# Merging column-tiled matmul groups and ordering a one-core decoder-layer kernel for late transfers

## Chip, cores and metric

One core of one Trainium2 chip runs the kernel. The metric is device microseconds of one execution; the time before is the median of 3 runs. TensorE is PE in the profile, VectorE DVE, ScalarE ACT, GpSimd POOL, and SyncE, which starts every transfer of this kernel, SP.

## What is computed

One decoder layer in float32 for a prompt of 512 tokens and 8 single-token samples, 520 token columns in all. Cut to what matters:

```python
mod = silu(c) @ w_ada + b_ada                       # shift, scale, gate; twice
h = modulate(rmsnorm(x), sh_m, sc_m)
u, z, xbc, dt_raw, g_a, g_b = split(h @ w_in)
ya, s5 states = s5_mixer(u, ...)                    # diagonal complex recurrence, 64 groups of 16 channels
yb, ssm states = ssd_mixer(z, xbc, dt_raw, ...)     # 32 heads of 64, chunks of 128 tokens
merged = sigmoid(g_a) * (ya @ w_branch_s5) + sigmoid(g_b) * (yb @ w_branch_ssd)
x = x + gt_m * rmsnorm(merged @ w_out)
gu = modulate(rmsnorm(x), sh_f, sc_f) @ w_ffn_in
x = x + gt_f * rmsnorm((silu(gu[:, :F]) * gu[:, F:]) @ w_ffn_out)
```

All new states (S5, SSM, convolution; of the prompt and of each sample) are outputs too.

## The kernel before, in words

Features lie on the 128 partitions, tokens along the free dimension. The **main stream** is the list of weight tiles of `build` (line 900): u, dt, the gates, then B, C, xs and z of four groups, glu, the two branches, w_out, w_ffn_in (fg, fu) and w_ffn_out (fo). A weight chunk is 128 output features by up to 1024 input features, 128x1024 words. It is loaded by SP (`wload`, line 858), rounded by ACT into `whi` (`wsplit_hi`, 863), its rest goes by DVE into `wlo` (`wsplit_lo`, 882), and PE multiplies it block of features by block (`product`, 1148): six passes of 260 token columns, hi and lo of the input on `whi`, and hi on `wlo`, for each half of the tokens. A chunk of eight blocks is 48 such passes. `whi` and `wlo` have three buffers each, so the split of a chunk can't start before PE is through with the chunk three places earlier.

Around it runs **side work**, written as Python generators: the S5 mixer (`s5` and helpers, 1731 to 2093), the SSD mixer (`ssd_unit`, 2247: two heads at a time, 16 units), the samples' outputs (`ssd_y`, 2321), their new states (`ssd_state`, 2369: 32 times a load `in_ssm`, three DVE operations of 128x512, a store), the last modulation (`ada_last`, 1350), and norms.

Three kinds of side matmuls use only some columns of the array. Their outputs go to 64 or 32 partitions, and the column groups work side by side:
- a unit's output, 64 columns, 14 matmuls; lines 2355 and 2362 (`if c % 2 == 0` and `if c % 2`) gather them in two bunches, of 6 and of 8;
- the samples' outputs, 32 columns, 32 matmuls for each of four head groups, in four bunches of 8, each on a 512 KB load `in_ssmT` (two buffers);
- the last modulation, 32 columns and 512 wide, eight bunches of 2.
The S5 and early modulation set-up has some more. A float32 matmul is two passes on the array, so two records in the trace.

No operation is issued when its helper is called. `Plan.add` records it with an estimated cost (from `mm`, `dma`, `act_cost` and so on) and with the memory it touches. At the end `Plan.order` (275) makes many schedules: `play` (352) runs all operations on a model of the engines, each engine taking the most urgent that can start; `back` (315) derives new priorities from the schedule run backwards; 24 rounds add random shifts to the priorities. The schedule with the earliest modelled end,
```python
end = max(o.fin for o in ops)
```
is issued, so each engine's instruction order is fixed when the program is built, and each engine then takes its instructions strictly in that order. A `bunch` (743) is one operation for the planner: nothing comes between its matmuls.

Of the kernel before, what the change touches and what calls it, by code (L numbers as in the profile page):

```python
# [46 lines left out]
PSTEP = 1 << 32  # L47


class Root:  # L50
    """A tile: `get` gives the real one (it may be made late); `loc` names the memory it lies in."""
# [14 lines left out]
class Ap:  # L66
    """A view of a tile: its shape and addresses at once, the real view when the operation is issued."""
# [65 lines left out]
    def cells(self):  # L133
        """Partitions, and the set of words in one of them (bits of an integer)."""
# [35 lines left out]
class Op:  # L170
    __slots__ = ("eng", "cost", "fn", "deps", "fset", "xfer", "start", "fin", "n", "nm", "pos", "prio", "main", "boost", "lead", "alt", "home", "nwait", "succ", "ready")

    def __init__(self, eng, cost, fn, deps, fset, xfer, boost=0.0):
        self.eng, self.cost, self.fn, self.deps, self.fset, self.xfer = eng, cost, fn, deps, fset, xfer
        self.nm, self.main, self.boost, self.alt, self.home = 1, False, boost, None, None


# delay in us from the end of an operation to the start of one that waits for it
# [7 lines left out]
class Line:  # L186
    """The time of one engine: busy stretches, into whose gaps operations are put."""
# [24 lines left out]
class Plan:  # L212
    """Records operations with the memory they touch, and orders them for the engines."""
# [51 lines left out]
    def remake(self, loc, fn, words):  # L265
        """The memory `loc` gets a new tile: after everything that used the old one."""
# [8 lines left out]
    def order(self):  # L275
        """The best of some schedules: by the longest way to the end, then by latest starts."""
# [20 lines left out]
        for r in range(NPERT + 1):  # L297
# [7 lines left out]
            for i in range(3 if r else NFB + 1):  # L305
                done = self.play()
                end = max(o.fin for o in ops)
# [7 lines left out]
    def back(self):  # L315
        """Priorities from the schedule played backwards: the time from an operation's latest start to the end."""
# [9 lines left out]
        while n < len(ops):  # L326
# [19 lines left out]
            for p, d in o.deps.items():  # L346
                rdy[p] = max(rdy[p], x + d)
# [4 lines left out]
    def play(self):  # L352
        """The course of the operations, each engine taking the most urgent of those that can start."""
# [8 lines left out]
        fset, cols, seen, pos = None, {}, {}, dict.fromkeys("VAGPSX", 0)  # L362
# [4 lines left out]
        while len(done) < len(ops):  # L367
# [47 lines left out]
            done.append(o)  # L415
            for s, d in o.succ:
                s.ready = max(s.ready, o.fin + d )
# [4 lines left out]

    def shift(self, t, free, cand):
        """An operation of DVE that ACT may take at time t, where that is done sooner."""
# [32 lines left out]
class Arena:  # L457
    """One run of words in a tile of one type; blocks are cut out of it first fit."""
# [39 lines left out]
class Mem:  # L498
    """A fixed float32 arena, and slots whose type (float32 or float32r) is chosen when one is empty."""
# [10 lines left out]
    def find(self, n, dt, top):  # L510
        """The place for n words: an arena index (0 = the fixed one), or None."""
# [89 lines left out]
class Builder:  # L601
# [76 lines left out]
    def relu(self, o, a, s):  # L678
        """max(a + s, 0)"""
# [18 lines left out]
    def dma(self, o, a, boost=0.0):  # L698
        """Starts a transfer; returns the estimate of its end."""
# [9 lines left out]
        c = n / run * max(.4375e-3, run * (1 if run >= 512 else 2) / 360e3)  # L709
# [6 lines left out]
    def mm(self, o, l, r, start=True, stop=True):  # L716
        n, m = self.fs(r), l.shape[-1]
        if l.dtype == F32R:
            c = max(n / 2400, .111) if m > 32 else .048
        else:  # L720
            c = max(n * 4 / 2400, .216) * max(m, 32) / 128 + (.021 if m <= 64 else 0.0)
        self.pe(c, lambda: self.nc.tensor.matmul(real(o), lhsT=real(l), rhs=real(r), start=start, stop=stop),  # L722
                [o], [l, r])

    def idle(self, o, n, after=None):
        """Matmuls on zeros."""
# [1777 lines left out]
```

## Time and profile before

| what | us |
|---|---|
| median of 3 runs | 1204.94 |
| the 3 runs | 1200.02, 1204.94, 1205.42 |
| profiled execution, span from first to last instruction | 1193.2 |
| median minus that span | 11.7 |
| PE busy | 1168.8 (98%) |
| DVE busy | 814.7 (68%) |
| ACT busy | 576.3 (48%) |
| PE's share of the chain that ended last | 79% |

The page gives the span of the profiled execution, not its whole time; what lies around a span is the 11.7 us of the table if that execution was like the median one. A PE record of a 260-column pass lasts about 0.28 us, while the next pass starts about 0.12 us after it: passes overlap, so work on PE is counted here by starts. An idle time that the profile states for PE begins at the end of the last record.

### The profile page before, as it was taken

The numbers are of one execution on the slowest core, as the hardware profiler recorded it, in microseconds if no ns is written. First come the engines' busy times: TensorE is split into PE (matmuls) and PEld (weight loads), VectorE is DVE, ScalarE is ACT, GpSimd is POOL, SyncE is SP. The second block draws the span as 40 slices with busy tenths as digits, with TensorE's granted clock in tenths as the row PEclk, the third lists the DMA queues.
The fourth block names the chain that finished last, engine by engine and source line by source line (L and its number), as shares of the span: only waits on it lengthen the run. The fifth ranks groups of instructions, "written<-read, shape, count | busy, mean of one in ns | idle before, by whom it ended". The sixth has DMA issues, their size and how long they took to land.

```text
span 1193.2 us, 24814 instructions
## 1 busy us (share of the span) xinstructions
PE 1168.8 (98%) x10182; PEld 1124.5 (94%) x10182; DVE 814.7 (68%) x1651; ACT 576.3 (48%) x981; POOL 4.9 (0%) x32
## 2 busy tenths in 40 slices
PE   8999999999999999999999999999999899999998
PEld 6899898999999999999998989999999899999997
DVE  6898989997696877868885435499576673322236
ACT  6655444357487657847853323465223222222233
POOL 0000000000000000000000000000000000000000
PEclk9999999999999999999999999999999999999999
DMA  8838698667243343355545674344566663223244
GB/s 292 278 119 219 162 215 224 180 160 208 82 134 101 114 128 125 116 175 169 188 145 201 241 268 144 129 166 147 182 217 203 198 206 104 88 81 97 83 130 135
DMA packets 118066, 195.49 MB, mean 164 GB/s; under 512 B 45856, under 2 KB 68800, under 8 KB 115648
## 3 DMA queue, kind: packets, MB, share of 16 engines
q1 hardware_dynamic: 117952, 193.90, 52.9%
q8 instruction: 80, 1.31, 0.4%
q14 instruction: 34, 0.28, 0.1%
HBM read 165.81 MB, written 23.86 MB: 159 GB/s over the span
## 4 chain that ended last, share of the span: by engine, by line
PE 79%; DMA 9%; DVE 7%; issue 1%; SPq 1%; ACT 1%; DVEq 0%; ACTq 0%
PE pm L722 64%; PE bank L722 14%; DVE s L640 4%; DMA arena<-in_ssm 3%; DVE arena L640 2%; PE bank L734 2%; DMA s<-in_w_as 1%; DMA out_ssm_s<-arena 1%; SPq L712 1%; DVE wlo L640 1%; DMA s<-in_w_in 1%; DMA ud<-s 1%; DMA s<-s 1%; DVE s L663 1%; ACT s L696 0%
## 5 line engine op out<-in xcount | busy, mean ns | idle before, releaser
L722 PE MATMUL pm<-hi,whi 128*128 128x260 f32 (+1 forms) x1856 | 497.5, 289 | 5.9 <-DVE arena L640 3.7
L722 PE MATMUL pm<-lo,whi 128*128 128x260 f32 (+1 forms) x1856 | 483.4, 282 | 0.0
L722 PE MATMUL pm<-hi,wlo 128*128 128x260 f32 x1840 | 370.4, 283 | 0.0
L722 PEld LDWEIGHTS pm<-hi,whi 128*128 128x128 f32 (+1 forms) x1856 | 349.6, 188 | 17.4 <-issue 13.0
L722 PEld LDWEIGHTS pm<-lo,whi 128*128 128x128 f32 (+1 forms) x1856 | 349.1, 188 | 0.1
L640 DVE TENSOR_TENSOR wlo<-arena,whi 128x1024 fp32r<-128x1024 f32 (+1 forms) x157 | 188.8, 1203 | 146.7 <-ACT whi L696 144.9
L722 PEld LDWEIGHTS pm<-hi,wlo 128*128 128x128 f32 x1840 | 282.9, 188 | 0.0
L696 ACT CAST whi<-arena 128x1024 fp32r<-128x1024 f32 (+1 forms) x158 | 162.6, 1029 | 197.1 <-PE pm L722 180.2
L722 PE MATMUL pm<-s,whi 128*128 128x260 f32 (+2 forms) x1128 | 184.2, 283 | 0.0
L640 DVE TENSOR_TENSOR arena<-arena 128x512 f32<-128x512 f32 (+11 forms) x299 | 140.3, 494 | 49.8 <-DMA arena<-in_ssm 29.4
L722 PEld LDWEIGHTS pm<-s,whi 128*128 128x128 f32 x1128 | 156.2, 188 | 5.1 <-issue 4.2
L722 PE MATMUL pm<-s,wlo 128*128 128x260 f32 (+2 forms) x564 | 117.2, 283 | 0.0
L722 PEld LDWEIGHTS pm<-s,wlo 128*128 128x128 f32 x564 | 88.1, 188 | 0.0
L691 ACT ACT_TABLE_LOAD x63 | 80.8, 1283 | 10.3 <-DMA s<-acd 3.5
L722 PE MATMUL bank<-s,s 128*64 128x128 f32 (+5 forms) x672 | 75.8, 282 | 5.6 <-ACT s L696 4.4
L722 PEld LDWEIGHTS bank<-s,s 128*128 128x128 f32 (+2 forms) x672 | 61.3, 164 | 10.9 <-ACT s L696 5.3
L691 ACT ACTIVATE s<-s 128x520 f32<-128x520 f32 (+10 forms) x89 | 50.0, 570 | 38.3 <-DVE s L640 17.7
L691 ACT ACTIVATE arena<-pm 128x260 f32<-128x260 f32 (+3 forms) x44 | 21.2, 489 | 92.7 <-PE pm L722 85.7
L640 DVE TENSOR_TENSOR s<-arena,s 128x520 fp32r<-128x520 f32 (+5 forms) x60 | 56.5, 948 | 10.6 <-ACT s L696 10.4
L640 DVE TENSOR_TENSOR s<-s,arena 128x8 f32<-128x8 f32 (+6 forms) x138 | 48.6, 369 | 13.8 <-ACT s L691 12.7
L722 PE MATMUL bank<-hi,s 128*128 128x260 f32 x256 | 55.5, 285 | 0.0
L722 PE MATMUL pm<-hi,s 128*128 128x260 f32 x256 | 55.0, 285 | 0.0
(122 smaller groups left out, 1265.8 us busy)
## 6 DMA issues: line engine op xcount, KB each, us to landing
arena<-in_w_in SPq DMA_DIRECT2D x59, 512.0 KB, 3.7
arena<-in_w_fi SPq DMA_DIRECT2D x44, 512.0 KB, 4.4
arena<-in_w_ada SPq DMA_DIRECT2D x12, 1024.0 KB, 7.5
arena<-in_w_fo SPq DMA_DIRECT2D x20, 512.0 KB, 3.6
arena<-in_ssmT SPq DMA_DIRECT2D x16, 512.0 KB, 4.4
s<-acd SPq DMA_DIRECT2D x16, 512.0 KB, 4.3
arena<-in_w_bssd SPq DMA_DIRECT2D x16, 512.0 KB, 5.4
arena<-in_ssm SPq DMA_DIRECT2D x32, 256.0 KB, 3.8
```

The lines of the kernel that those rows point to most:

```text
L640: self.op("V", .068 + self.fs(o) / 960, lambda: self.nc.vector.tensor_tensor(out=real(o), in0=real(a), in1=real(b), op=op), [o], [a, b, *a ...
L663: self.op("V", .068 + self.fs(o) / 960, lambda: self.nc.vector.tensor_tensor_scan(out=real(o), data0=real(a), data1=real(b), initial=0.0, ...
L691: self.op("A", c, lambda: self.nc.scalar.activation(real(o), real(a), f, bias=real(bias), scale=real(scale)), [o], [a, scale, bias], None ...
L696: self.op("A", c, lambda: self.nc.scalar.copy(real(o), real(a)), [o], [a])
L712: p = self.op("S", .475 if same else .65, lambda: self.nc.sync.dma_start(out=real(o), in_=real(a)), [o], [a], None, c)
L722: self.pe(c, lambda: self.nc.tensor.matmul(real(o), lhsT=real(l), rhs=real(r), start=start, stop=stop), [o], [l, r])
L734: self.pe(.108, lambda: self.nc.tensor.transpose(real(o), real(a), real(d)), [o], [a, d])
```

## The change

It does four things. (1) The matmuls of a unit's output are one bunch of 14 instead of 6 and 8; those of the samples' outputs come in bunches of 16 instead of 8; those of the last modulation in bunches of 4 instead of 2. The two loads that feed a bunch of the latter two kinds are both waited for, and the next two are started after it. (2) The planner charges PE 0.09 us where the number of columns in use changes, and gives an operation with the same narrow tile a bonus of 4 us in urgency. (3) Estimates: a 260-column pass costs 0.120 us instead of 0.108, transfers go at 330 instead of 360 GB/s, and whoever waits for a transfer is planned 1 us later. (4) Of the schedules, the one with the best mean end over six rehearsals is taken, in which the order is fixed and each transfer is late by a random time of mean 0.5 us. The arithmetic, the transfers and the number of matmuls stay as they are.

```diff
+RATE = 330e3
+WAIT = 1.0
+LATE = .5
+NREH = 6
+NSW = .09
+TSTAY = 4.0
...
             for i in range(3 if r else NFB + 1):
                 done = self.play()
-                end = max(o.fin for o in ops)
+                end = self.rehearse(done)
...
             for p, d in o.deps.items():
-                rdy[p] = max(rdy[p], x + d)
+                rdy[p] = max(rdy[p], x + d + (WAIT if p.eng == "S" else 0.0))
...
+            elif e == "P":
+                o = max(c, key=lambda o: (o.prio + (TSTAY if o.tile == tile != 128 else 0.0), -o.n))
+                if o.tile != tile:
+                    t += NSW
+                    tile = o.tile
...
+            late = WAIT if e == "S" else 0.0
             for s, d in o.succ:
-                s.ready = max(s.ready, o.fin + d )
+                s.ready = max(s.ready, o.fin + d + late)
...
+    def rehearse(self, done):
...
+        for r in range(NREH):
+            rnd = random.Random(r)
+            fin, free, lanes = [], dict.fromkeys("VAGPSXQ", 0.0), [0.0] * 8
+            for e, c, deps, wt, load, xfer, lane in rows:
+                t = free[e] + load
...
+                if e == "S":
+                    t = max(t, dep, lanes[lane]) + c
+                    free[e] = t
+                    t = free["Q"] = max(free["Q"], t + .65) + xfer
+                    t += rnd.expovariate(1 / LATE)
+                    lanes[lane] = t + .95
+                else:
+                    t = max(t, dep + wt) + c
+                    free[e] = t
+                fin.append(t)
+            total += max(fin)
+        return total / NREH
...
-        c = n / run * max(.4375e-3, run * (1 if run >= 512 else 2) / 360e3)
+        c = n / run * max(.6e-3, run * (1 if run >= 512 else 3) / RATE)
...
-            c = max(n / 2400, .111) if m > 32 else .048
+            c = max(n * .441e-3 + .005, .112)
...
-        for n in range(8):
+        for n in range(1, 8, 2):
             e, q = 10 + n // 4, n % 4
-            yield ts[n % 2]
-            if q == 0:
+            yield max(ts)
+            if q == 1:
                 p = yield from self.pget()
             with self.bunch():
-                for i in range(2):
-                    j = 2 * (q % 2) + i
-                    self.mm(p[32 * j:32 * j + 32, :], self.sc[:, 2 * q + i, :], bufs[n % 2][:, i], start=(q < 2), stop=(q > 1))
+                for h in (q - 1, q):
+                    for i in range(2):
+                        j = 2 * (h % 2) + i
+                        self.mm(p[32 * j:32 * j + 32, :], self.sc[:, 2 * h + i, :], bufs[h % 2][:, i], start=(h < 2), stop=(h > 1))
             yield 0
             if n < 6:
-                ts[n % 2] = load(n + 2)
+                ts = [load(n + 1), load(n + 2)]
...
-            if c % 2 == 0:
+            if c == 0:
                 self.group = []
...
-            if c % 2:
-                self.ungroup()
-                yield "c"
+        self.ungroup()
...
-            for j in range(4):
-                yield ts[j % 2]
+            for j in (0, 2):
+                yield max(ts)
                 with self.bunch():
-                    for b in range(2 * j, 2 * j + 2):
+                    for b in range(2 * j, 2 * j + 4):
...
-                    ts[j % 2] = load(4 * g + j + 2)
+                    ts = [load(4 * g + j + 2), load(4 * g + j + 3)]
```

Since costs and choice change, the whole order changes, on every engine. Three places show it. In the rows a name in front of `<-` is what is written, `pm` and `bank` are PSUM, `x4` counts equal instructions in a row, and lines of the change are 56 higher.

PE, a unit's output in the SSD stage, before:

```order
L722 MATMUL pm_69<-hi,wlo_74 128x260 x2
L722 MATMUL bank_65<-s_15_684,s_24_3413 64x128 x4
L722 MATMUL bank_65<-arena,s_24_3413 64x128 x2
L722 MATMUL pm_69<-hi,whi_71 128x260
L722 MATMUL pm_69<-lo,whi_71 128x260
L722 MATMUL pm_69<-hi,whi_71 128x260
L722 MATMUL pm_69<-lo,whi_71 128x260
L722 MATMUL pm_69<-hi,wlo_74 128x260 x2
L722 MATMUL bank_65<-s_15_684,s_24_3413 64x128 x2
L722 MATMUL bank_65<-arena,s_24_3413 64x128 x2
L722 MATMUL bank_65<-s_15_684,s_24_3413 64x128 x2
L722 MATMUL bank_65<-arena,s_24_3413 64x128 x2
```

and a unit's output in the changed order:

```order
L778 MATMUL pm_69<-hi,wlo_75 128x260 x2
L778 MATMUL bank_68<-s_15_700,s_24_3569 64x128 x4
L778 MATMUL bank_68<-arena,s_24_3569 64x128 x2
L778 MATMUL bank_68<-s_15_700,s_24_3569 64x128 x2
L778 MATMUL bank_68<-arena,s_24_3569 64x128 x2
L778 MATMUL bank_68<-s_15_700,s_24_3569 64x128 x2
L778 MATMUL bank_68<-arena,s_24_3569 64x128 x2
L778 MATMUL pm_70<-hi,whi_73 128x260
```

The six matmuls and the eight that stood apart, with one block of the main stream between, are 14 in a row now. All 16 units stand so; before, 10 of them were split.

SP, from the last part of the start on; `in_w_in` and `in_w_dt` are weight chunks, `dtd` is the scratch of the SSD mixer's dt, and the 128x8x64 write to `ud` begins the exchange through memory with which S5's first unit starts. Before:

```order
L712 DMA arena<-in_w_in 128x1024 x4
L712 DMA dtd<-s_14_682 256x1x128
L712 DMA dtd<-s_14_682 256x1x2
L712 DMA s_13_579<-dtd 32x2x130 x4
L712 DMA arena<-in_w_in 128x1024
L712 DMA ga_82<-s_16_997 128x520
L712 DMA s_11_133<-in_s5m 128x512
L712 DMA arena<-in_w_in 128x1024
L712 DMA ga_83<-s_18_1108 128x520
L712 DMA ud_80<-s_14_682 128x8x64
```

and now:

```order
L768 DMA arena<-in_w_in 128x1024
L768 DMA s_11_133<-in_s5m 128x512
L768 DMA s_10_134<-in_s5hx 128x8x8
L768 DMA s_11_133<-in_s5hx 128x8x8
L768 DMA out_cso<-arena 3072x1x16
L768 DMA arena<-in_w_dt 128x256
L768 DMA s_11_133<-in_s5hy 128x64
L768 DMA arena<-in_w_in 128x1024 x2
L768 DMA ud_80<-s_14_699 128x8x64
```

The write to `ud` comes after eight chunks now instead of twelve, and ahead of the dt scratch. PE's first multiplication that depends on it (128x72) moves the other way: it stands after 884 passes of the main stream, where it stood after 692.

SP, the end of the samples' states, in the w_ffn_in stage (`in_w_fi`); before:

```order
L712 DMA arena<-bcd_105 128x128
L712 DMA out_ssm_s<-arena 128x512
L712 DMA arena<-in_ssm 128x512 x2
L712 DMA arena<-in_w_fi 128x1024
L712 DMA out_ssm_s<-arena 128x512
L712 DMA arena<-in_w_fi 128x1024
L712 DMA out_ssm_s<-arena 128x512
L712 DMA arena<-in_w_fi 128x1024 x9
```

and now:

```order
L768 DMA arena<-in_ssm 128x512
L768 DMA out_ssm_s<-arena 128x512
L768 DMA arena<-in_w_fi 128x1024
L768 DMA arena<-in_ssm 128x512
L768 DMA out_ssm_s<-arena 128x512
L768 DMA arena<-in_w_fi 128x1024
L768 DMA out_ssm_s<-arena 128x512
L768 DMA arena<-in_w_fi 128x1024 x5
```

Nine weight chunks followed the last store before, five follow now; the 32 loads `in_ssm` are spread over 27 weight loads instead of 24, from first to last.

## Rows read from the trace of the kernel before

**Rows 1.** The page: span, busy times, and the chain that ended last by engine.
```profile
span 1193.2 us, 24814 instructions
...
PE 1168.8 (98%) x10182; PEld 1124.5 (94%) x10182; DVE 814.7 (68%) x1651; ACT 576.3 (48%) x981; POOL 4.9 (0%) x32
...
PE 79%; DMA 9%; DVE 7%; issue 1%; SPq 1%; ACT 1%; DVEq 0%; ACTq 0%
```

**Rows 2.** Stretches: from:to, length, busy PE, PEld, DVE, ACT, POOL, PEclk, DMA share, GB/s.
```profile
0.00:28.00 28.00, 23.44 (x237) 18.61 (x237) 17.76 (x78) 16.34 (x43) 1.41 (x8) 1.00 0.89 298
28.00:40.00 12.00, 10.18 (x86) 8.08 (x79) 6.63 (x18) 8.97 (x20) 0.18 (x3) 1.00 0.98 386
40.00:245.00 205.00, 195.94 (x1713) 188.92 (x1712) 186.84 (x415) 101.19 (x239) 2.94 (x20) 0.99 0.73 188
245.00:610.00 365.00, 365.00 (x3426) 352.33 (x3425) 291.56 (x652) 251.21 (x360) 0.39 (x1) 1.00 0.46 140
...
845.00:955.00 110.00, 105.87 (x884) 105.48 (x883) 74.72 (x102) 28.83 (x37) 0.00 (x0) 1.00 0.63 201
...
1158.00:1193.20 35.20, 30.36 (x232) 28.51 (x230) 20.75 (x44) 14.00 (x26) 0.00 (x0) 0.98 0.46 144
```

**Rows 3.** Waits of PE, the largest sum: us in total, times, longest.
```profile
PE bank L722 <- ACT s L696: 6.2, 4, 1.9
```

**Rows 4.** Timeline of PE: a unit's output that stood whole (28 passes); start, us.
```profile
402.04 0.40 PE L722 MATMUL pm<-hi,wlo 128*128 128x260 f32 x2
402.37 0.66 PE L722 MATMUL bank<-s,s 128*64 128x128 f32 x8
...
404.05 0.39 PE L722 MATMUL pm<-hi,whi 128*128 128x260 f32 x1
404.27 0.28 PE L722 MATMUL pm<-lo,whi 128*128 128x260 f32 x1
```

**Rows 5.** The same, a unit's output in two parts (12 and 16 passes).
```profile
409.83 0.40 PE L722 MATMUL pm<-hi,wlo 128*128 128x260 f32 x2
410.15 0.66 PE L722 MATMUL bank<-s,s 128*64 128x128 f32 x8
...
411.18 0.28 PE L722 MATMUL pm<-lo,whi 128*128 128x260 f32 x1
...
411.55 0.40 PE L722 MATMUL pm<-hi,wlo 128*128 128x260 f32 x2
411.88 0.44 PE L722 MATMUL bank<-s,s 128*64 128x128 f32 x4
...
413.13 0.28 PE L722 MATMUL pm<-lo,whi 128*128 128x260 f32 x1
```

**Rows 6.** Timeline of PE after its wait at 130.90.
```profile
130.90 1.12 PE L734 MATMUL bank<-arena 128*128 128x128 f32 x4 [1.70 <-DVE s L667]
...
132.03 0.42 PE L722 MATMUL pm<-lo,whi 128*128 128x260 f32 x1
132.25 0.42 PE L722 MATMUL pm<-hi,whi 128*128 128x260 f32 x1
```

**Rows 7.** One stretch, just after that wait; columns as in rows 2.
```profile
131.50:133.60 2.10, 2.10 (x12) 2.10 (x11) 2.04 (x4) 0.78 (x2) 0.00 (x0) 0.50 0.74 195
```

**Rows 8.** Timeline of DVE around the wait at 952.
```profile
947.41 1.22 DVE L640 TENSOR_TENSOR wlo<-arena,whi 128x1024 fp32r<-128x1024 f32 x1
952.48 1.42 DVE L640 TENSOR_TENSOR arena<-arena 128x512 f32<-128x512 f32 x2 [3.85 <-DMA arena<-in_ssm]
```

**Rows 9.** Timeline of PE around the wait at 954.
```profile
950.58 0.41 PE L722 MATMUL pm<-hi,wlo 128*128 128x260 f32 x2
954.65 0.36 PE L722 MATMUL pm<-hi,whi 128*128 128x260 f32 x1 [3.67 <-DVE arena L640]
```

**Rows 10.** One stretch, DVE's 16th to 32nd split of a whole chunk; columns as in rows 2.
```profile
147.95:279.76 131.81, 126.72 (x1118) 123.97 (x1117) 123.66 (x225) 64.17 (x141) 1.14 (x10) 1.00 0.78 194
```

**Rows 11.** Transfers by tensor: count, KB each, median us from issue to landing.
```profile
arena<-in_ssmT SPq DMA_DIRECT2D x16, 512.0 KB, 4.4
```

More of the change, by code (lines that the diff above doesn't have):

```diff
@@ L170 @@
 class Op:
-    __slots__ = ("eng", "cost", "fn", "deps", "fset", "xfer", "start", "fin", "n", "nm", "pos", "prio", "main", "boost", "lead", "alt", "home", "nwait", "succ", "ready")
+    __slots__ = ("eng", "cost", "fn", "deps", "fset", "xfer", "start", "fin", "n", "nm", "pos", "prio", "main", "boost", "lead", "alt", "home", "nwait", "succ", "ready", "idx", "tile")
     def __init__(self, eng, cost, fn, deps, fset, xfer, boost=0.0):
         self.eng, self.cost, self.fn, self.deps, self.fset, self.xfer = eng, cost, fn, deps, fset, xfer
-        self.nm, self.main, self.boost, self.alt, self.home = 1, False, boost, None, None
+        self.nm, self.main, self.boost, self.alt, self.home, self.tile = 1, False, boost, None, None, 128
 DELAY = {("V", "V"): .127, ("V", "A"): .128, ("V", "G"): .155, ("V", "P"): .256, ("V", "S"): .12,
@@ L361, in play @@
         lanes = [0.0] * 8
-        fset, cols, seen, pos = None, {}, {}, dict.fromkeys("VAGPSX", 0)
+        fset, cols, seen, pos, tile = None, {}, {}, dict.fromkeys("VAGPSX", 0), 128
         for o in ops:
@@ L421, in play @@
         return done
+    def rehearse(self, done):
+        for i, o in enumerate(done):
+            o.idx = i
+        rows, seen, pos, fset, tile = [], {}, dict.fromkeys("VAGPSX", 0), None, 128
+        for o in done:
+            e, w = o.eng, {}
+            for p in o.deps:
+                if p.eng not in (e, "X"):
+                    q = p.eng + str(p.pos % 8) if p.eng == "S" else p.eng
+                    if p.pos > seen.get((e, q), -1):
+                        w[q] = max(w.get(q, -1), p.pos)
+            for q, i in w.items():
+                seen[e, q] = i
+            load = 0.0
+            if e == "A" and o.fset not in (None, fset):
+                load, fset = 1.283, o.fset
+            if e == "P" and o.tile != tile:
+                load, tile = NSW, o.tile
+            rows.append((e, o.cost, [(p.idx, d) for p, d in o.deps.items()], .117 * (len(w) // 2), load, o.xfer, o.pos % 8))
+        total = 0.0
+        for r in range(NREH):
[3 more added lines that the diff above has]
+                t = free[e] + load
+                dep = 0.0
+                for i, d in deps:
+                    x = fin[i] + d
+                    if x > dep:
+                        dep = x
+                if e == "S":
[10 more added lines that the diff above has]
+        return total / NREH
     def shift(self, t, free, cand):
@@ L733, in tp, with pe @@
         d = self.ident[:n, :n]
-        self.pe(.108, lambda: self.nc.tensor.transpose(real(o), real(a), real(d)), [o], [a, d])
-    def pe(self, c, fn, outs, ins):
+        self.pe(.112, lambda: self.nc.tensor.transpose(real(o), real(a), real(d)), [o], [a, d])
+    def pe(self, c, fn, outs, ins, tile=128):
         if self.group is None:
-            self.op("P", c, fn, outs, ins)
+            self.op("P", c, fn, outs, ins).tile = tile
         else:
             self.group.append((c, fn, outs, ins))
+            self.gtile = tile
     @contextmanager
@@ L752, in ungroup @@
                     sum([x[2] for x in g], []), sum([x[3] for x in g], []))
-        o.nm = len(g)
+        o.nm, o.tile = len(g), self.gtile
     def main(self):
@@ L2337, in ssd_y @@
             p = yield from self.pget()
-            for j in range(4):
-                yield ts[j % 2]
+            for j in (0, 2):
+                yield max(ts)
                 with self.bunch():
-                    for b in range(2 * j, 2 * j + 2):
+                    for b in range(2 * j, 2 * j + 4):
                         for i in range(4):
                             self.mm(p[32 * i:32 * i + 32, 0:128], cm[:, 32 * b:32 * b + 32],
-                                    hs[j % 2][:, b % 2, 128 * i:128 * i + 128], start=(b == 0), stop=(b == 7))
+                                    hs[b // 2 % 2][:, b % 2, 128 * i:128 * i + 128], start=(b == 0), stop=(b == 7))
                 if 4 * g + j + 2 < 16:
-                    ts[j % 2] = load(4 * g + j + 2)
+                    ts = [load(4 * g + j + 2), load(4 * g + j + 3)]
             self.mm(p[:, 128:136], self.ones, self.bcs[:, g, 1])
```

4 lines of the change are left out of this document (2 added, 2 removed).

## The prediction

> **What bounds the kernel now.** I read the page first, then a table of stretches, then the waits and the timeline around them. The page [rows 1] says PE: it is busy 98% of the span and holds 79% of the chain that ended last; DVE has 68%. The stretches [rows 2] say where PE isn't busy: up to 40 us, where the transfers bound it (DMA share 0.89 and 0.98); from 40 to 245, where S5 is set up (9.06 us idle, with DVE busy 186.84 of 205); from 845 to 955, the samples' states (4.13 us); and in the tail (4.84 us). From 245 to 610 it has no idle time at all. So the change can gain in two ways: fewer microseconds of PE's own work, or fewer waits.
>
> How much waits can give needs a choice of meter. PE's own row leaves 24.4 us of the span idle, PEld's 68.7 [rows 1]. From 245 to 610 PE is never idle, yet PEld lacks 12.65 us of the 365 [rows 2]: what PEld lacks isn't all waiting. I cap the waits by PE. The Trainium skill (Perfetto Trace Analysis, Identifying the Most-Contended Engine) says the opposite: matmul busy time is a bad measure because matmuls are pipelined, and weight-load busy time is the one to use. By that rule up to 68.7 us would be open and my sum would be no upper bound; the stretch without idle time speaks against it here, and I give little chance to more than the idle time that is listed below.
>
> All sums are made on the profiled execution, span 1193.2 us; the median is 11.7 above that span, and I subtract from the median, 1204.94. A single kernel measurement of this kind tells about 0.5%, 6 us, from no change.
>
> **Part 1, merged groups.** A unit's output that stood whole: from the start of the last pair of main passes at 402.04 to the second main pass after it at 404.27 it is 2.23 us [rows 4]. Three of those steps are main passes at 0.12 us (one lasts 0.28 and a pair 0.40, so the second starts 0.12 after the first), and the output itself takes 1.87. In two parts: 411.18 - 409.83 - 0.36 = 0.99 and 413.13 - 411.55 - 0.36 = 1.22 [rows 5], together 2.21. The passes are the same 28, so one more run of column-tiled passes costs 0.34 us of PE time. Entering it is plain in the rows: the pair starts at 409.83, its second pass at 409.95, and the first narrow pass 0.20 later instead of 0.12.
>
> How many runs go? The trace holds 71 of them, and the changed order 53: unit outputs 26 to 16, samples' outputs 13 to 8, last modulation 5 to 4, S5 set-up and earlier modulation 27 to 25. That is 18 x 0.34 = 6.1 us, all of it on PE, the bound engine. Lower bound: only the entrance, 0.08 us a run, 1.4 us. I take 6.1, since rows 4 and 5 are the very operation that is merged.
>
> What the merges cost: a unit's first six matmuls now wait until the last state of the recurrence is there, and a PSUM bank is held by one bunch. Nobody waits for the first half alone, since the addition to the skip term reads all of it. For the samples' outputs the two 512 KB loads start only after both are used, so their 4.4 us to landing [rows 11] is no longer under the other buffer's matmuls. Cover: the closest such groups in the changed order stand 66 main passes apart, 66 x 0.12 = 7.9 us, and PE had no idle time in that stretch [rows 2]. I set it at nothing; if the cover were gone, each of the 8 reloads could cost up to 4.4. The same holds for the last modulation, 72 passes apart.
>
> **Part 2, S5 set-up, 40 to 245.** The waits here are of side matmuls on ACT and DVE [rows 3, 6]: PE's fixed order had put S5's multiplications before their data could be there. Of the 9.06 us idle, 5.09 lie in the stretch from 147.95 to 279.76 [rows 10], so 3.97 lie before it. Each wait hides 0.16 more: the gap of 3.67 at 954.65 is 954.65 - 950.70 = 3.95 between starts, 0.12 of which is usual [rows 9]. Three waits: 0.5. After the third, at 130.90, the granted clock is 0.50 for 2.1 us [rows 7], the lower level of 1.2 GHz; passes start 0.22 apart [rows 6], so about 1.05 is lost. Sum 5.5 us. In the change the first S5 multiplication stands 192 passes (four chunks, 23 us) later on PE, and the write it descends from is four chunks earlier on SP. So these waits should go: -5.5.
>
> The other 5.09 I leave standing. DVE does the densest part of S5 there: 223 operations between its 16th and 32nd split, busy 123.66 of 131.81 [rows 10]. The changed order has the same number, 223, between the 18th and 33rd, 15 chunks instead of 16. PE has one chunk less of main passes (5.8) to cover the same DVE work, so waits on DVE are as near as before.
>
> **Part 3, samples' states, 845 to 955.** DVE waited 3.85 us for a load `in_ssm`, with the next split queued behind it [rows 8]; PE then stood for 3.67 [rows 9]. With 0.46 elsewhere the stretch lost 4.13, and 0.3 hidden. The changed order spreads the 32 loads over 27 chunks instead of 24: 27 x 5.76 / 32 = 4.86 us a load instead of 4.32, 17 us more in all. I take 3.4 off and keep 1.0, since DVE still takes these operations strictly in turn.
>
> **Start, tail, SP.** In the start a 512 KB weight load moves ahead of two 1 MB modulation loads, 1.36 us at 386 GB/s [rows 2]; PE's wait there, 1.82 us in 28 to 40, may grow or shrink by that. Nothing, with bounds of 1.8 either way. The tail has the same operations; nothing, 0.5 either way. The numbers of transfers and instructions are unchanged; new constants cost no instruction.
>
> **Sum.** 6.1 + 5.5 + 3.4 = 15.0; 1204.9 - 15.0 = **1190 us**. If all the waits listed went, 6.1 + 5.5 + 5.7 + 4.4 = 21.7, 1183 (5.7 is the 5.09 with 0.16 for each of its four waits).
>
> **Rivals.**
> - *The waits come back elsewhere.* The old order, too, was chosen for the earliest modelled end and then met 14 us of waits, since the data came later than planned. A one-microsecond allowance covers transfers [rows 8], not the waits on ACT and DVE [rows 3]. Then only Part 1 is left: 1204.9 - 6.1 = 1198.8, 1196 to 1203.
> - *A run costs only its entrance.* 1.4 instead of 6.1, waits as forecast: 1194.6. Rows 4 and 5 speak against it.
> - *DVE becomes the bound in S5's dense part; slower.* Place: the 15 chunks between DVE's 18th and 33rd split. PE needs 131.81 - 5.09 - 5.76 = 121 us for them, and the three buffers let DVE be two chunks behind, 11.5 more: 132.5. DVE's work there is some 122 us (nearly the mix of rows 10), which at the 94% of rows 10 takes 130: no loss, by 2.5 us. At 86% it would be 142, a loss of 9.3: 1199. From 80% on, 152.5, the loss is over 20 us, which eats the gain and 6 us besides. At 77% it is 158, a loss of 26: 1216, slower. For it: in the changed order DVE has three chunks with nothing but their splits just ahead of that part, so the work can't be drawn forward. Against it: in no part of rows 10 is DVE so empty.
> - *The change doesn't do what it says.* The order shows that the merges are made; what is left is that lateness isn't what stalls PE, which is the first rival.
>
> **Chances.** Forecast 0.48; waits come back 0.26; entrance only 0.10; DVE as the bound 0.11; more than all listed gone, below 1184, 0.05. Faster by over 0.5% means under 1198.9: 0.46 of the first, 0.09 of the second, 0.10 and 0.05, so 0.70. Slower, over 1211: 0.09, of the DVE case. The same: the remaining 0.21. The range from 1184 to 1205 leaves out 0.05 below, and above it the DVE case and a little of the second, 0.15.
>
> **What would show it.** Right: tiled runs fall to 53 and a unit's output takes 1.87 us everywhere; PE's idle time from 40 to 245 falls to about 5 and that from 845 to 955 to about 1; no stretch with granted clock 0.50 near 130. Wrong: PE waits on DVE's split of weights in the dense part of S5, around 150 to 290 us, or the idle time of the samples' states is as large as before. If PE's idle time falls by 8 us or more and the time doesn't, the step that failed is the meter chosen at the start.

## The result, and the profile after

The changed kernel takes **1190.21 us** (median of 4 runs, 1188.48 to 1191.52) against 1205.18 for the kernel before (1200.02 to 1207.75): ratio 0.9885, 95% interval 0.9862 to 0.9909. Its profiled execution took 1189.08 us with a span of 1187.0, so 2.1 us lie around the span.

The page after, lines as in [rows 1]:
```profile
span 1187.0 us, 24824 instructions
...
PE 1165.4 (98%) x10182; PEld 1126.7 (95%) x10182; DVE 812.4 (68%) x1638; ACT 574.1 (48%) x991; POOL 4.8 (0%) x32
...
PE 73%; DVE 8%; issue 2%; ACT 1%; DMA 1%; DVEq 0%; SPq 0%; ACTq 0%
```
The stretches after, columns as in [rows 2]:
```profile
0.00:28.00 28.00, 23.27 (x236) 18.30 (x237) 18.09 (x80) 16.73 (x45) 1.41 (x8) 1.00 0.92 304
28.00:40.00 12.00, 11.95 (x96) 9.83 (x95) 7.61 (x17) 8.87 (x19) 0.18 (x3) 1.00 0.99 390
40.00:245.00 205.00, 199.50 (x1759) 193.63 (x1758) 178.09 (x396) 99.98 (x228) 2.76 (x19) 1.00 0.72 180
245.00:610.00 365.00, 361.24 (x3417) 352.75 (x3417) 303.11 (x667) 250.85 (x383) 0.43 (x2) 0.99 0.49 150
...
735.00:845.00 110.00, 108.09 (x884) 105.03 (x883) 81.60 (x171) 55.92 (x115) 0.00 (x0) 1.00 0.42 138
845.00:955.00 110.00, 110.00 (x922) 110.00 (x922) 71.75 (x97) 30.43 (x39) 0.00 (x0) 1.00 0.62 190
...
1158.00:1187.00 29.00, 23.31 (x162) 20.75 (x160) 16.54 (x38) 9.54 (x20) 0.00 (x0) 0.94 0.40 124
```
Read against [rows 2]: PE's idle time from 40 to 245 fell from 9.06 to 5.50 us, and that of the samples' states, 845 to 955, from 4.13 to nothing. But 3.76 us are idle now between 245 and 610, where there were none, 1.91 between 735 and 845, likewise, and the tail is idle for 5.69 instead of 4.84. In all PE's idle time fell by only 2.8 us. These are the two longest new waits, on PE's timeline after (in brackets: idle before, and its releaser):
```profile
215.18 1.11 PE L778 MATMUL bank<-s,s 128*128 128x72 f32 x8 [2.84 <-ACT s L752]
...
249.08 3.69 PE L778 MATMUL bank<-s,s 128*128 128x72 f32 x16 [3.31 <-ACT s L752]
252.51 0.57 PE L778 MATMUL pm<-hi,whi 128*128 128x260 f32 x1
```
Both are S5 multiplications that stand on PE ahead of their data, of the same kind as the waits that are gone.

A unit's output after, on the same timeline:
```profile
425.22 0.40 PE L778 MATMUL pm<-hi,wlo 128*128 128x260 f32 x2
425.55 0.66 PE L778 MATMUL bank<-s,s 128*64 128x128 f32 x8
...
427.23 0.39 PE L778 MATMUL pm<-hi,whi 128*128 128x260 f32 x1
427.45 0.28 PE L778 MATMUL pm<-lo,whi 128*128 128x260 f32 x1
```
427.45 - 425.22 = 2.23, as in [rows 4]; all 16 units stand whole, and the trace holds 53 tiled runs instead of 71.

Before any experiment one thing in these numbers doesn't fit. The two spans differ by 6.2 us and the two medians by 15.0.

### The profile page after: what moved, and what is told of

Same layout as the page of the kernel before. It is cut to its first block, busy times and chain, and to the rows that moved or that the text cites. A ratio compares the mean times of both kernels' runs of the same rounds, so it can differ in the third digit from the quotient of the medians.

```text
span 1187.0 us, 24824 instructions
## 1 busy us (share of the span) xinstructions
PE 1165.4 (98%) x10182; PEld 1126.7 (95%) x10182; DVE 812.4 (68%) x1638; ACT 574.1 (48%) x991; POOL 4.8 (0%) x32
## 4 chain that ended last, share of the span: by engine, by line
PE 73%; DVE 8%; issue 2%; ACT 1%; DMA 1%; DVEq 0%; SPq 0%; ACTq 0%
PE pm L778 61%; PE bank L778 11%; DVE s L696 4%; DVE arena L696 1%; PE bank L790 1%; DVE s L707 1%; DMA s<-in_s5m 1%; ACT arena L747 0%; DMA s<-yd 0%; DVE arena L707 0%; DVE s L719 0%; DVE wlo L696 0%; DVE lo L707 0%; ACT L747 0%; DVE arena L716 0%
## 5 line engine op out<-in xcount | busy, mean ns | idle before, releaser
L778 PEld LDWEIGHTS pm<-hi,whi 128*128 128x128 f32 (+1 forms) x1856 | 349.7, 188 | 10.5 <-issue 7.8
L696 DVE TENSOR_TENSOR arena<-arena 128x512 f32<-128x512 f32 (+12 forms) x299 | 140.9, 496 | 46.1 <-ACT arena L747 21.5
L778 PEld LDWEIGHTS bank<-s,s 128*128 128x128 f32 (+2 forms) x680 | 64.5, 168 | 10.1 <-ACT s L752 7.2
L747 ACT ACTIVATE s<-s 128x520 f32<-128x520 f32 (+10 forms) x94 | 53.6, 575 | 33.5 <-DVE s L696 15.9
L747 ACT ACTIVATE arena<-pm 128x260 f32<-128x260 f32 (+3 forms) x43 | 20.6, 486 | 88.4 <-PE pm L778 86.1
L696 DVE TENSOR_TENSOR s<-s,s 128x512 f32<-128x512 f32 (+9 forms) x94 | 57.4, 616 | 4.9 <-ACT s L747 3.2
L696 DVE TENSOR_TENSOR arena<-arena,pm 128x520 f32<-128x520 f32 x26 | 18.1, 695 | 57.1 <-PE pm L778 57.0
```

Source lines behind the costliest of these rows:

```text
L696: self.op("V", .068 + self.fs(o) / 960, lambda: self.nc.vector.tensor_tensor(out=real(o), in0=real(a), in1=real(b), op=op), [o], [a, b, *a ...
L747: self.op("A", c, lambda: self.nc.scalar.activation(real(o), real(a), f, bias=real(bias), scale=real(scale)), [o], [a, scale, bias], None ...
```

## The experiments

All kernels were timed beside the kernel before, whose median in these sessions was 1202.66 to 1205.18 us; a ratio or a difference below is to the kernel before of the same session. The table takes each profiled execution apart; the experiments are told below it. *Idle* is PE's idle time between its first and last matmul. *Low clock* is what PE loses at the lower of its two levels, 1.2 instead of 2.4 GHz: in the view of stretches, cut into pieces of 1 us, one minus the granted clock, times PE's busy time, summed. *Work* is PE's busy time less that. *Tiled runs* counts the unbroken rows of passes of one narrow tile on PE; the main stream's own 64-column passes (dt) and single passes of 8 columns are left out.

| kernel | median | profiled execution, span | idle | low clock | work | tiled runs |
|---|---|---|---|---|---|---|
| before | 1205.18 | 1193.2 | 19.3 | 1.4 | 1167.4 | 71 |
| before again (e1) | 1205.31 | 1203.3 | 20.6 | 7.7 | 1169.9 | 71 |
| changed | 1190.21 | 1187.0 | 16.8 | 4.6 | 1160.8 | 53 |
| changed again (e5) | 1190.64 | 1188.4 | 15.9 | 6.7 | 1160.6 | 53 |
| e2 old order, joined | 1199.17 | 1200.0 | 22.1 | 10.0 | 1162.8 | 61 |
| e3 new order, split | 1195.54 | 1193.5 | 16.5 | 4.9 | 1166.4 | 68 |
| e4 merges only | 1201.40 | 1198.0 | 21.5 | 11.1 | 1160.1 | 55 |
| e6 group later | 1190.12 | 1190.2 | 15.1 | 11.4 | 1158.8 | 53 |
| e7 planner only | 1195.13 | 1192.6 | 16.6 | 6.8 | 1164.3 | 54 |
| e8 no lateness | 1203.75 | 1198.4 | 23.8 | 6.2 | 1162.5 | 53 |
| e9 other draw | 1190.97 | 1189.1 | 15.8 | 8.2 | 1159.8 | 53 |
| e10 no lateness, other draw | 1199.59 | 1199.7 | 23.3 | 10.4 | 1160.7 | 53 |
| e11 lateness doubled | 1190.25 | 1189.2 | 17.7 | 5.9 | 1160.9 | 53 |
| e12 tail late | 1186.94 | 1182.8 | 13.7 | 3.4 | 1160.7 | 53 |

### e1 and e5: both kernels again, unchanged

> The kernel before, unchanged, for a second profile. Theory A: the profiled execution of before (span 1193.2 us) was shorter than its timed runs (1200.0 to 1207.8), because late transfers make PE wait more in most executions; then this run's median is 1203 to 1207, the spans of its runs spread over 5 us or more, and a second profile shows waits on transfers that the first did not. Theory B: the timed runs are longer than the profile by a fixed part that lies outside the span; then the span stays within 2 us of 1193 and the time is some 11 us above it.

> The changed kernel, unchanged, for a second profile. The second profile of before was 10.1 us longer in span than the first, with three stretches at a granted clock of 0.50 behind waits before 1000 us instead of one. Theory A: the changed order meets fewer and shorter waits on transfers, so its executions are alike; then the span is 1186 to 1190, PE's idle gaps sum to 15 to 18 us, and one stretch of clock 0.50 stands behind the wait near 249. Theory B: the first profile of the changed kernel was a lucky one too; then the span is 1193 or more, with new waits before 1000 us.

Theory A holds in e1's times: the median is 1205.31, and the spans spread over 5.4 us. e1's profiled execution took 1205.26 with a span of 1203.3, so what lies around a span is 2 us here too, and before's first profile was of an execution of about 1195: shorter than every timed one. The same instructions in the same order took 10.1 us longer. Theory A's cause holds in part: the waits are the same ones, some of them longer, and of the 10.1 us only 1.3 are idle time; 6.3 are low clock, and 2.5 lie in the work column. The two timelines of PE show the waits; first before, then e1 (the same wait in S5), then e1 (samples' states):
```profile
202.37 1.11 PE L722 MATMUL bank<-s,s 128*128 128x72 f32 x8 [1.86 <-ACT s L696]
```
```profile
205.60 1.98 PE L722 MATMUL bank<-s,s 128*128 128x72 f32 x8 [3.20 <-ACT s L696]
...
963.36 0.56 PE L722 MATMUL pm<-hi,whi 128*128 128x260 f32 x1 [4.56 <-DVE arena L640]
963.71 0.42 PE L722 MATMUL pm<-lo,whi 128*128 128x260 f32 x1
```
The eight passes take 1.98 instead of 1.11 us in e1, where the clock is low. The wait at 963 answers to the 3.67 of [rows 9]. Behind three of e1's waits the clock is low; its stretches, columns as in [rows 2] (PEclk is the number behind the POOL column):
```profile
131.60:138.00 6.40, 6.38 (x33) 6.38 (x33) 5.02 (x12) 1.47 (x6) 0.00 (x0) 0.56 0.67 139
205.60:213.00 7.40, 7.40 (x37) 7.40 (x38) 4.40 (x11) 2.47 (x7) 0.23 (x2) 0.54 0.90 259
963.30:967.00 3.70, 3.64 (x18) 3.67 (x19) 3.63 (x6) 0.57 (x1) 0.00 (x0) 0.54 0.51 126
```
In the first profile only one such stretch stood, [rows 7]. So a wait has two prices, its length and, in some executions, a low-clock stretch behind it, and the pair that compares typical executions is e1 against e5: work -9.3, idle -4.7, low clock -1.0, together 15.0, where the spans differ by 14.9.

The changed order is the steadier one, as e5's Theory A had it: its two profiles are 1.4 us apart, and PE's idle time is 15.9. But it has more than the one low-clock stretch that Theory A expected. It has low-clock stretches behind the wait at 249, in the tail (see e12) and, in e5 alone, behind a wait of 1.06 us at 791; the first and the last of these in e5:
```profile
248.70:256.00 7.30, 7.25 (x35) 7.25 (x36) 7.19 (x16) 3.14 (x12) 0.00 (x0) 0.53 0.61 159
791.00:795.00 4.00, 3.95 (x20) 3.85 (x20) 4.00 (x9) 3.15 (x7) 0.00 (x0) 0.57 0.00 0
```

### e2 and e3: what a tiled run costs

e2 is before with the first bunch of each split unit issued right ahead of the second:
```diff
+        for i, o in enumerate(done):
+            k = getattr(o.fn, "unit", None)
+            if k and k[1] == 0:
...
+                    held[k[0]] = o.fn
+                    continue
+            if k and k[0] in held:
+                held.pop(k[0])()
```
e3 is the changed kernel with a unit's last 8 matmuls issued after the main operation that follows:
```diff
+            if getattr(o, "parts", None):
+                for f in o.parts[:6]:
+                    f()
+                late = (o, lambda fs=o.parts[6:]: [f() for f in fs])
+                continue
...
+            if late and o.eng == "P" and o.main:
+                late[1]()
```


> Order of before; the 10 split unit outputs are made whole by issuing the first half right ahead of the second; nothing else moves. If a column-tiled run costs 0.34 us: 10 fewer runs, 3.4 us off, about 1201.8 by a median of 1205.2. If a run costs only its entrance, 0.08: 0.8 us, 1204.4. In the trace the outputs that stood in two parts take 1.87 us instead of 2.21.

> Order of the changed kernel; the last 8 matmuls of about 15 unit outputs are issued after the main operation that follows, so that each is two runs again; nothing else moves. If a run costs 0.34 us: 15 more runs, 5.1 us more, about 1195.3 by a median of 1190.2. If it costs only its entrance: 1.2 us, 1191.4.

e2: ratio 0.9964 (0.9945 to 0.9983), so 4.3 us off for 10 runs (2.0 to 6.6). e3: 1195.54, ratio 0.9927 (0.9909 to 0.9945) where the changed kernel has 0.9885 and, again, 0.9896 (0.9881 to 0.9911): 3.7 to 5.1 us more for 15 runs. Both stand with 0.34 a run (0.43; 0.25 to 0.34). The entrance alone, 0.8 and 1.2 us, is outside e2's interval and at the low end of what e3 allows: with both intervals taken together, its shift is, by an estimate, 1.5 us or more by the first timing of the changed kernel and 0.9 or more by the second. The traces decide. An output that e2 joined, and one that stood split in e3, read like [rows 4] and [rows 5]:
```profile
416.62 0.41 PE L722 MATMUL pm<-hi,wlo 128*128 128x260 f32 x2
...
418.64 0.39 PE L722 MATMUL pm<-hi,whi 128*128 128x260 f32 x1
418.86 0.28 PE L722 MATMUL pm<-lo,whi 128*128 128x260 f32 x1
```
```profile
427.22 0.40 PE L778 MATMUL pm<-hi,wlo 128*128 128x260 f32 x2
...
428.58 0.28 PE L778 MATMUL pm<-lo,whi 128*128 128x260 f32 x1
...
428.94 0.40 PE L778 MATMUL pm<-hi,wlo 128*128 128x260 f32 x2
...
430.52 0.29 PE L778 MATMUL pm<-lo,whi 128*128 128x260 f32 x1
```
418.86 - 416.62 - 0.36 = 1.88 us for the joined one, and 1.00 + 1.22 for the split one, so the run costs 0.34 in both orders. Two runs of the samples' outputs cost 0.33 us more than one, in the same way. A straight line through the work of all fourteen executions gives 0.41 us a run, 7.4 us for the 18 of the change; that is rougher, since the work of one kernel differs by 2.5 us between before and e1. The Trainium skill (TensorEngine Tiling (Array Packing), Key Properties) says that changing the tiling mode drains the engine. The delays at both ends of a run are in keeping with that; no run here shows the drain itself.

### e4 and e7: the merges without the planner, the planner without the merges

e4 is before with these three hunks of the change, e7 the changed kernel with them undone (in the kernel before, the lines `if c % 2 == 0` and `if c % 2` are 2297 and 2306, not 2355 and 2362):
```diff
-        for n in range(8):
+        for n in range(1, 8, 2):
...
-            if c % 2 == 0:
+            if c == 0:
...
-            for j in range(4):
-                yield ts[j % 2]
+            for j in (0, 2):
+                yield max(ts)
```


> Before with the three merges alone and the old planner: about 59 runs instead of 71, and the old planner draws a new order of its own. If the merges bring their runs and nothing else: 12 x 0.34 = 4.1 us off, 1201. If most of the 15 us comes from the merges: 1195 or less. If the old planner's order meets other waits than before: anything from 1196 to 1208, with PE idle before 245 us of 8 us or more in the profile.

> The changed planner with the three merges undone. It joins most unit halves by itself: 56 runs instead of 71. If the tile bonus does what the merges do, and the order is as good: 15 x 0.34 = 5.1 us off for runs, and the waits as in the changed kernel, 1190 to 1193. If the merges matter for more than their runs: 1196 or more.

e4: ratio 0.9980 (0.9963 to 0.9996), 2.4 us off; it has 55 runs, not 59. The merges brought their work, 1160.1 as in the changed kernel, and the old planner's new order gave much of that back: idle and low clock are 32.6 us instead of e1's 28.3. So 1201, the sum for the merges alone, came true by two errors that cancel: the runs saved more than was said, and the waits rose. e7: 0.9936 (0.9918 to 0.9953), 7.7 us off, between its two expectations. Its waits are about those of the changed kernel, 23.4 us against e5's 22.6; its work is 3.7 us higher. One more run at 0.34 doesn't explain that; the last modulation does. A bunch of it in the changed kernel (8 passes), and one in e7 (4 passes):
```profile
738.78 1.06 PE L778 MATMUL bank<-arena 128*32 128x512 f32 x8
```
```profile
744.64 1.05 PE L778 MATMUL bank<-arena 128*32 128x512 f32 x4
```
The four passes fill two of the four column groups and last as long as the eight that fill all four. The changed kernel has four bunches of 8; e7 has one of 8 and six of 4, three bunches more at about 1.18 us each with entering and leaving: 3.5 us. So the planner joins a unit's halves by itself, and the merge of the last modulation is what it lacks in e7.

### e8, e9, e10, e11: planning for late transfers, and luck

The order comes out of a search with random shifts, so one order proves little. e8 takes the lateness out, e9 only starts the search elsewhere, e10 does both, e11 doubles the lateness (WAIT 2.0, LATE 1.0). This is e10's edit; its first part alone is e9's, its second e8's:
```diff
-SEED = 149
+SEED = 150
...
-WAIT = 1.0
-LATE = .5
+WAIT = 0.0
+LATE = 1e-6
```


> The changed kernel with the lateness of transfers taken out of the planner: no 1 us allowance and no drawn lateness; merges, tile bonus and new durations stay. 54 runs. If planning for late transfers is what cuts the waits: work as in the changed kernel, waits and low clock as in before's second profile (28 us instead of 21), so 1195 to 1199. If it is the luck of the search or the new durations: within 3 us of the changed kernel, 1187 to 1193.

> The changed kernel with another start of the random search for the order; nothing else. The order found is another, so this tells how much of the gain is the luck of one order. If the planner's treatment of late transfers is what pays: 1188 to 1196, PE's idle gaps and time lost at the lower clock together 20 to 25 us. If the changed kernel's order was a lucky find: 1198 to 1206, and 27 us or more.

> As the run without lateness, with the other start of the search. That run came out at 1203.8, 13 us above the changed kernel, with the same work on PE. If the lateness in the planner is what pays: 1197 to 1206 again, idle gaps and clock 27 to 33 us. If the one without lateness was an unlucky find: 1188 to 1195.

> The changed kernel with twice the lateness in the planner: 2 us allowed for each transfer, 1 us on average drawn in the rehearsals. If orders get better the more lateness they allow for: 1184 to 1189. If half of that was enough and more pushes transfers into earlier memory and other waits: 1188 to 1196. No theory says over 1200.

With lateness planned for: 0.9885 and 0.9896 (the changed kernel), 0.9895 (e9; 0.9875 to 0.9915), 0.9886 (e11; 0.9864 to 0.9907). Without: 1.0007 (e8; 0.9996 to 1.0019) and 0.9960 (e10; 0.9944 to 0.9975). All six executions stand at 53 runs and at work of 1159.8 to 1162.5. Between kernels timed side by side, e8 against e5 and e10 against e9, the lateness is worth 13 and 8 us, at least as much as the merges, and it isn't the luck of one draw. e8 keeps the new durations and the charge and bonus for narrow tiles, so these don't carry the gain by themselves. Without the lateness the merged kernel is as slow as before in one draw and 5 us faster in the other, in spite of 5 to 9 us less work on PE. Idle and low clock of e9 sum to 24.0, of e10 to 33.7, each near what was expected. Twice the lateness brings no more. e8 came out slower than either of its expectations. Its profiled execution was the shortest of its ten (1200.22), so its 30.0 us of idle and low clock are a low value.

What the planner did with it shows best in the samples' states. Waits of DVE between 840 and 970 us for the loads `in_ssm` (us in total, times, longest), first before, then changed, e8, e10:
```profile
DVE arena L640 <- DMA arena<-in_ssm: 26.7, 15, 5.0
```
```profile
DVE arena L696 <- DMA arena<-in_ssm: 13.1, 8, 5.0
```
```profile
DVE arena L696 <- DMA arena<-in_ssm: 35.3, 20, 4.9
```
```profile
DVE arena L696 <- DMA arena<-in_ssm: 37.7, 19, 4.5
```
And PE, which waits behind DVE there, in e8 and in e10 (whole span):
```profile
PE pm L778 <- DVE arena L696: 6.3, 5, 2.1
```
```profile
PE pm L778 <- DVE arena L696: 5.9, 3, 4.5
```
In the changed kernel that sum is 0.5. The order of SP shows why: from the first to the last of the 32 loads it starts 22 weight loads in e8 and 23 in e10, 24 in before, but 28 in the changed kernel and 27 in e9. PE's idle time from 845 to 990 us is 5.9 in both e8 and e10 and nothing in the changed kernel and e9. The fixed allowance, the late draws and the choice by rehearsal were taken out together; which of the three does it wasn't tried.

### e6: one long wait taken away

The two S5 bunches that wait at 249.08 go six main groups later, on PE alone:
```diff
+        pe = [o for o in done if o.eng == "P"]
+        tg = [o for o in pe if o.s72][which:which + 2]
...
+        pe[i:j + 1] = pe[i + 2:j + 1] + tg
```


> The changed kernel; only on PE, the two bunches of 128x72 matmuls that waited 3.31 us near 249 us stand six main groups (36 passes, 4.3 us) later. Theory A: a wait costs its own length and, behind it, a stretch at clock 0.50 (3.0 us in the changed kernel's profile); then both go and the time is 6 us under the changed kernel's, about 1184. Theory B: the low clock there doesn't come from the wait; then only 3.3 goes, 1187. Theory C: what waits for these matmuls on DVE and ACT is late in turn and PE waits elsewhere by as much; then no change, 1190.

Theory C: 1190.12, no change (ratio 0.9892, 0.9873 to 0.9911, or 1187.4 to 1192.0 us, which leaves out A and, narrowly, B). Ahead of the place this execution stands 3.6 us behind the changed kernel's first one (the same main pass starts at 237.75 and 234.18); once the passes and the two bunches are through it stands 2.2 ahead (255.81 and 258.04). So 5.8 us were gained. Then what hangs on these matmuls is late, and a main group waits for ACT's copy of a bank, with a low-clock stretch (columns as above):
```profile
249.70 0.39 PE L778 MATMUL pm<-hi,whi 128*128 128x260 f32 x1 [0.37 <-ACT s L747]
...
260.89 0.39 PE L778 MATMUL pm<-hi,whi 128*128 128x260 f32 x1 [2.68 <-ACT s L752]
```
```profile
217.40:224.50 7.10, 7.06 (x34) 7.06 (x35) 6.96 (x14) 2.52 (x6) 0.45 (x4) 0.52 0.84 214
260.90:266.00 5.10, 5.10 (x30) 5.10 (x31) 5.10 (x9) 2.70 (x5) 0.00 (x0) 0.67 0.20 63
```
The 2.68 and 1.7 lost at the lower clock give back 4.4 of the 5.8. The first of these rows has nothing to do with the edit: this execution lost 3.4 us more behind the wait at 217.

### e12: the tail

On PE, four of the five preloads of the last sums go behind the last main pass:
```diff
+        pe = [o for o in done if o.eng == "P" and o.tail != 1]
+        i = max(k for k, o in enumerate(pe) if o.tail == 2) + 1
+        pe[i:i] = [o for o in done if o.eng == "P" and o.tail == 1]
```


> The changed kernel; on PE, four of the five preloads of the last sums (8 passes of 128x256) stand behind the last main passes, where PE waits for the last norm, as they do in before, instead of between main passes. In the changed kernel's profile they take 0.67 + 1.42 us there, with a wait of 0.47, and the gap behind the main passes is 1.7 us. If the gap covers them: 1.3 to 2 us off, about 1188.7 by a median of 1190.4. If the low clock in the tail makes them end after the gap: no change.

1186.94 us, ratio 0.9857 (0.9834 to 0.9879), the best version of all, though its interval overlaps that of the changed kernel. The trace shows where it gains. The changed kernel's preloads between main passes (0.67 us from the first row on, 1.42 from the second to the next main pass), its gap behind them, and the clock of its last 3.5 us:
```profile
1156.92 1.02 PE L778 MATMUL pm<-arena 128*128 128x256 f32 x4
...
1165.99 0.60 PE L778 MATMUL bank<-arena 128*128 128x256 f32 x2
1167.06 0.70 PE L778 MATMUL pm<-arena 128*128 128x256 f32 x2 [0.47 <-ACT arena L747]
...
1178.18 0.71 PE L778 MATMUL bank<-arena 128*128 128x128 f32 x4 [1.10 <-DVE arena L702]
```
```profile
1179.90:1183.40 3.50, 3.50 (x9) 2.20 (x8) 2.87 (x9) 1.49 (x4) 0.00 (x0) 0.52 0.33 109
```
The same in e12:
```profile
1171.92 0.61 PE L778 MATMUL bank<-arena 128*128 128x1 f32 x4 [0.47 <-ACT arena L752]
1172.39 1.11 PE L778 MATMUL pm<-arena 128*128 128x256 f32 x4
1173.34 0.59 PE L778 MATMUL bank<-arena 128*128 128x256 f32 x2
1173.77 0.59 PE L778 MATMUL pm<-arena 128*128 128x256 f32 x2
1174.20 1.04 PE L778 MATMUL bank<-arena 128*128 128x256 f32 x6
```
```profile
1175.70:1179.20 3.50, 2.93 (x10) 1.65 (x10) 3.41 (x11) 1.53 (x5) 0.00 (x0) 1.00 0.34 112
```
The eight passes now fill the gap, and the clock stays at its upper level to the end. From the last main pass's start to the last matmul's end it takes 1179.13 - 1171.17 = 7.96 us, with the preloads, where the changed kernel takes 1183.43 - 1175.72 = 7.71 without them; the 0.67 + 1.42 us among the main passes are saved. So the edit is worth about 1.8 us, as forecast; the other 2.4 of the 4.2 us between the two profiled spans aren't shown to be its doing: e12 also met a shorter wait in S5 (2.03 us at 214 instead of 2.84 at 215).

## Why the prediction was right, and where it wasn't

The time, 1190.2, is the forecast of 1190, and the gain came by the two ways it named, less work on PE and fewer waits. Not every step to it held, and that it came out to the microsecond is luck in part: from e1 to e5 work fell by 9.3 where 6.1 were said, and idle time and low clock by 5.7 where 8.9 were said. Both add up to 15.0.

**The base of the sum failed.** "The median is 11.7 above that span, and I subtract from the median" took 11.7 us for something that stays. It is 2.0 us around the span and some 10 us of luck: before's profiled execution met one low-clock stretch where e1's met three, and shorter waits. The waits were read from that lucky execution and the sum subtracted from the median of ordinary ones. On its own ground, the profiled pair, 15.0 off a span of 1193.2 would have been 1178; it was 1187.0.

**Part 1 held, a little small.** 71 to 53 runs, as counted. 6.1 us was said; the work column gives 6.6 for the first pair, 9.3 for e1 and e5, and 7.4 by the line through all executions. One price for all 18 runs was wrong: the one that went from the last modulation brought 1.2 us, a whole bunch (see e7), and not 0.34. Read run by run in the first two traces, the unit outputs give 3.5, the samples' outputs 1.7, the last modulation 1.2 and the set-up 0.6, together about 7.0. The rival of 1.4 us falls with e2 and e3. The covers that were named held as well: PE has no wait on `in_ssmT` in either profile of the changed kernel. (What PEld lacks from 245 to 610 is 12.67 us by [rows 2], not 12.65; nothing hangs on it.)

**Part 2, half.** The waits before 147.95 went, but for 0.85 at 108.5, and so did the low-clock stretch of [rows 7]. What was to be left standing, the waits in the dense part of S5, went too, and others came in their place: 2.84, 1.07 and 3.31 us (at 215, 227 and 249), with 3.0 us of low clock, against 5.09 in [rows 10]. That waits in this part are "as near as before" was right, though by the profile the longest two end on ACT and not on DVE; that the new ones cost a low-clock stretch was not in the sum. In e1, before's own waits there were 1.33, 0.85, 3.20 and 1.57, with a low-clock stretch too.

**Part 3 held, and more.** PE's wait is gone, not 1.0 left. e1 lost 4.56 there and the low-clock stretch behind it. The spread of the loads, which the forecast named as the cause, goes with the wait in all of before, the changed kernel, e8, e9 and e10 (the changed kernel spreads them over 28 weight loads, not 27).

**Start and tail were mis-sized.** Idle from 28 to 40 fell from 1.82 to 0.05, the upper bound, though 0 was taken; e1 and e5 have 1.70 and 0.43. The tail was set at 0 with 0.5 either way; e12 shows that the planner's new place for the preloads cost 2.1 us among the main passes, and a low-clock stretch at the end.

**The rivals.** "The waits come back elsewhere" is what the first pair of profiles shows: beyond the first 20 us, nine waits over 0.7 us each went, 14.5 us together, and six came, 10.2. For it spoke that an allowance for transfers doesn't cover waits on ACT and DVE. e8 and e10 answer that for DVE alone. PE's waits on DVE sum to 13.6 and 14.5 us there, against 4.2 and 4.3 in the changed kernel's two profiles, as DVE itself stands longer behind transfers (43.0 and 43.5 us against 25.3 and 24.6). PE's waits on ACT are no longer without the allowance (6.7 and 5.8 against 10.5 and 8.6). DVE as the bound was not seen in any run: the dense part's waits are on single S5 operations, and DVE's split of weights is not among PE's longer waits.

**The meter.** The Trainium skill (Perfetto Trace Analysis, Identifying the Most-Contended Engine) names weight-load busy time as the measure of TensorE's headroom, beside the share of peak arithmetic, and not matmul busy time. The two traces agree: from e1 to e5 the span less PEld fell from 71.1 to 59.7 (page rows 1203.3 and 1132.2, 1188.4 and 1128.7), 11.4 of the 14.9 us; PE's idle time fell by 4.6. What a tiled run costs lies in PE's busy time: e3, which differs from e5 by fifteen runs, has 65.3 us of its span without PEld and e5 59.7, while PE's idle time differs by 1.2. PE's idle time caps the waits alone, and only as a cap on them was it used.

## What to carry to other kernels

Take two profiles of the kernel before, and only then put a price on its waits: an order of instructions that waits on transfers can differ by 10 us between executions, and one profile may be of the shortest. A planner that fixes the order should plan for transfers that come late; that was worth 8 and 13 us here, as much as the merged matmuls saved or more. Narrow matmuls should be gathered until they fill all column groups, since half-filled bunches took as long as full ones. Small matmuls that don't hang on the last main pass belong in the gap behind it, where they cost 0.25 us here instead of 2.1 and the clock stayed at its upper level.

## What the runs showed of the hardware

**A wait's second price isn't set by its length.** With the same order, PE waited 2.84 us at 215 in the changed kernel and kept the full clock behind it; in e6 it waited 2.38 at the same place and then ran 7 us at a granted clock of 0.52. The wait of 1.06 us at 791 had a low-clock stretch behind it in e5 and none in the changed kernel's first profile; before's 3.67 at 954 had none, e1's 4.56 had one. What decides between them is open.

**A run of narrow passes costs 0.34 us, of which 0.08 shows at its entrance.** The starts of the single passes that [rows 4] and [rows 5] sum up tell where it lies. The first narrow pass starts 0.20 to 0.21 instead of 0.12 us after the pass ahead, and the second pair of narrow passes 0.05 later than the pairs behind it. At the other end the first main pass starts 0.10 later than one more narrow pair would, and the second main pass 0.22 instead of 0.12 after the first. Each later pair adds 0.11 us, whatever the run's length.

**Two column groups took as long as four.** Bunches of 32 columns and 512 wide lasted 1.05 us with four passes on two column groups and 1.06 us with eight passes on four.
